# Mixer arithmetic moved from GpSimd to VectorE, up to the queries of a hybrid decoder layer

## The chip, the core and the metric

The kernel runs on one core of one Trainium2 chip. The metric is the device time of one execution in microseconds (us), lower is better. In the views of the profile PE is TensorE's matmul, PEld its weight load, DVE is VectorE, ACT is ScalarE, POOL is GpSimd, and SP is the queue that issues most DMAs. L191 is line 191 of the kernel before.

## What is computed

One decoder layer on 512 tokens of width 1,024, in float32. `c` is one vector that modulates the norms.

```python
mod = silu(c) @ w_ada + b_ada                      # six vectors of 1024
sh1, sc1, gt1, sh2, sc2, gt2 = split(mod, 6)
h = rms_norm(x, norm1_w) * (1 + sc1) + sh1
p = h @ w_in                                       # u, v; q, k, v, z; a, b
y_a = gelu(u) * spatial_gating(gelu(v))            # 8 heads, chunks of 128
q, k, v = silu(short_conv(p_q, p_k, p_v))          # 4 taps, then l2 norm of q, k
y_b = rms_norm(gated_delta_rule(q, k, v, g(a), beta(b))) * silu(z)   # 4 heads
x = x + gt1 * (concat(y_a, y_b) @ w_out)
h2 = rms_norm(x, norm2_w) * (1 + sc2) + sh2
x = x + gt2 * peer(h2)     # queries, keys, top 16, 128^2 single-neuron experts
out = rms_norm(x, final_norm_w)
```

The delta rule is computed chunkwise. Each chunk of 128 tokens needs the inverse of a unit triangular matrix for each of four heads.

## The kernel before, in words

Activations lie transposed, 128 channels on the partitions and 512 tokens along the row, eight such tiles for the width of 1,024. Every projection is made of three matmuls per tile: a float32 operand is split into an upper part (`hi`, a rounding cast on ScalarE) and a remainder (`lo = full - hi`, `split_lo`, L83), and `mm3` (L78 to L80) adds hi x hi, lo x hi and hi x lo. `weights` (L125) loads a block of 128 output columns as 128 x 1,024, casts it on ScalarE (L129) and forms the remainder on GpSimd unless another engine is named. Three buffers each hold `raw`, `whi` and `wlo`.

The stages, in order:

- *First norm* (L206 to L274). VectorE makes seven level masks `lvl` with 28 small instructions, adds up squares, and reduces sixteen rows of `w_ada` against silu(c) (`mod_sums`, L201, tiles of 128 x 1,024 called `wada`, eight buffers). The inverse root comes back as one row `rr`, the same on all partitions. GpSimd multiplies `xT` by `rr` (L253). For each of the eight tiles two sums are advanced, VectorE adds the bias and forms a scale column and a shift column, ScalarE writes `hhi` and once more the same value unrounded (`full`), and `low_parts` forms `hlo`, on GpSimd for four of the eight tiles (`GPL`). VectorE's order is as written here; the other engines' order is the planner's.
- *Convolution stage* (L308 to L408). Twelve projections of q, k and v go through `conv_silu`: a ScalarE copy, one L189 and three L191 on VectorE, a silu. Between them stand `lengths` (transposes and sums of squares, L354), the decay scalars (L325 to L339) and `decays` (`ml` and `att` on GpSimd, `LS` on VectorE). The order of TensorE is written by hand (`ORD`); the planner orders VectorE, ScalarE, GpSimd and the DMAs.
- *Chunk comparison* (L412 to L434): the triangular matrices `LS` and the attention matrices `att`, four chunks, between them the rest of the projections of v.
- *Levels of the inverse* (L446 to L471). Seven levels; per level and chunk a masked product `ms` on GpSimd (L451), then `py`, `pz`, `px` on TensorE and the updates of `X` and `Z` on VectorE. Thirty of the remaining 32 sums of `w_ada` are put among them, with two `wada` buffers.
- *Delta rule, gating and output projection* (L477 to L658), with `kd`, `sd`, the normed heads `on` and the masked gating weights on GpSimd; remainders of the mixed tiles alternate between VectorE and GpSimd (`split_mixed`).
- *Second norm* (L668 to L694): for tiles 2, 4 and 6 ScalarE scales `x2T` first (`pre`) and GpSimd multiplies by the row; the other tiles take one VectorE instruction.
- *Queries, routing and experts* from L763 on. The queries' weight remainders stay where they are, on GpSimd but for two.

Of the kernel before, what the change touches and what calls it, by code (L numbers as in the profile page):

```python
# [10 lines left out]
F32 = mybir.dt.float32  # L11
# [9 lines left out]
P = 128  # L21
D = 1024
S = 512
# [18 lines left out]
LATE = 1  # L42
ORD = "q1 l0 k2 q2 d l1 k3 l2 q3 f l3".split()
PRE2 = (2, 4, 6)
# [6 lines left out]
GPL = (2, 4, 5, 6)  # L51
# [8 lines left out]
def layer(ctx: ExitStack, tc: tile.TileContext, I, out):  # L60
# [64 lines left out]
    def weights(pl, src, n, eng=None):  # L125
        raw = pl.tile([P, KD, n], F32, tag="raw", name="raw")
        nc.sync.dma_start(raw, src)
        hi = pl.tile([P, KD, n], F32R, tag="whi", name="whi")
        nc.scalar.copy(hi, raw)  # L129
        lo = pl.tile([P, KD, n], F32R, tag="wlo", name="wlo")  # L130
        split_lo(eng or nc.gpsimd, lo, raw, hi)
        return hi, lo

# [9 lines left out]
    with ExitStack() as mixer:  # L143
# [52 lines left out]
        def mod_sums(which, wad, dst, base=0):  # L196

            for c in which:
                w = wad.tile([P, D], F32, tag="wada", name="wada")
                nc.sync.dma_start(w, I["w_ada_c"][c])  # L200
                nc.vector.tensor_tensor_reduce(w, w, scB, scale=1.0, scalar=0.0, op0=OP.mult, op1=OP.add,  # L201
                                               accum_out=dst[:, c - base:c - base + 1])
# [3 lines left out]
        with ExitStack() as n1, tc.manual_schedule(engines={nc.vector.engine}):  # L206
            for l in range(7):
                nc.vector.tensor_scalar(sj, pi, l, None, op0=OP.logical_shift_right)
                nc.vector.tensor_scalar(si, fi, l, 1, op0=OP.logical_shift_right, op1=OP.bitwise_xor)
                same = zT[:, 0, :P]  # L210
                nc.vector.tensor_tensor(same, si, sj, op=OP.is_equal)
                nc.vector.scalar_tensor_tensor(lvl[:, l], same, -1.0, m2[:, 0], op0=OP.mult, op1=OP.mult)
# [5 lines left out]
            wk0 = weights(wst, I["w_in_t"][4], P)  # L218
            ahead = mod_sums([8 * (1 - i) + k for k in range(KD) for i in range(2)], wad, mod)
# [16 lines left out]
            wq0 = weights(wst, I["w_in_t"][0], P, nc.vector)  # L236
# [4 lines left out]
            split_lo(nc.gpsimd, wlo, raw, whi)  # L241
            if not LATE:
                advance(ahead, 2)
# [8 lines left out]
            for k in range(KD):  # L252
                nc.gpsimd.tensor_tensor(xT[:, k], xT[:, k], rr, op=OP.mult)  # L253
                if k == 1:
                    wk1 = weights(wst, I["w_in_t"][5], P)
            fulls = []

            def low_parts(k):
                split_lo(nc.gpsimd if k in GPL else nc.vector, hlo[:, k], fulls[k], hhi[:, k])

            for k in range(KD):
                scale, shift = sc[:, k:k + 1], mod[:, k:k + 1]
# [12 lines left out]


        with ExitStack() as gdn, tc.manual_schedule(engines={nc.tensor.engine}):
# [90 lines left out]
            def decays(n):  # L368

                ml, ex = X[n], Y[n]  # L370
                nc.gpsimd.tensor_tensor(ml, bc(later[:, None, :], HP), col(g, n), op=OP.mult)
# [5 lines left out]
                nc.gpsimd.tensor_tensor(att[n], ex, bc(m2[:, 1:2], HP), op=OP.mult)  # L377
# [816 lines left out]
```

## Time and profile before

| | |
|---|---|
| median of 3 runs | 1,665.87 us (1,664.70 to 1,669.69) |
| profiled execution | 1,667.16 us, its span 1,665.5 us |
| PE busy | 1,567.7 us, 94% of the span |
| DVE busy | 1,311.7 us, 79% |
| ACT busy | 647.2 us, 39% |
| POOL busy | 662.6 us, 40% |

The span is the time from the first to the last instruction of the profiled execution. Busy shares are averages over stages that have different limits; the matmuls' ends are modelled, and they overlap, so that starts tell more than ends. In a row of the timeline stand start, length, engine, line, operation, output and inputs, the count, and in brackets how long the engine had been idle and what ended that.

### The profile page before, as it was taken

To read this page: it belongs to the slowest core of one execution; us is meant where nothing else is said; L and a number is where in the kernel's file an instruction comes from. 1 tells how busy PE (TensorE), PEld (TensorE's weight loads), DVE (VectorE), ACT (ScalarE), POOL (GpSimd) and SP (SyncE) were. 2 spreads that over 40 slices of the span, in tenths; PEclk is the share of its full clock that TensorE was granted. 3 is DMA by queue.
4 is the path that set the end of the run, shared out by engine and by line. 5 is a ranking of instruction groups with operands and counts; after the bars stand their busy time and mean duration, and the time that the engine had idled before them with its cause. 6 is when DMAs were issued, how large, how long until landed. Compare 5 with 4: busy or idle time off the path is not lost.

```text
span 1665.5 us, 23058 instructions
## 1 busy us (share of the span) xinstructions
PE 1567.7 (94%) x8567; PEld 1382.2 (83%) x8567; DVE 1311.7 (79%) x2388; ACT 647.2 (39%) x931; POOL 662.6 (40%) x454
## 2 busy tenths in 40 slices
PE   4889989999998889997999999999999999999996
PEld 2568988877888889986888888888888888888884
DVE  9889872545999999983688887888888888887755
ACT  4542123435335545553333333333333333333333
POOL 5455543426435610001244444445444444544201
PEclk9989999999999999998999999999999999999998
DMA  7311561236204457777889999999999999999753
GB/s 283 122 65 55 193 207 51 89 111 208 88 26 140 150 192 284 274 267 263 301 312 340 346 349 318 339 349 353 310 352 328 361 330 328 350 355 317 245 188 124
DMA packets 133396, 402.31 MB, mean 242 GB/s; under 512 B 12450, under 2 KB 49186, under 8 KB 131619
## 3 DMA queue, kind: packets, MB, share of 16 engines
q1 hardware_dynamic: 95106, 261.89, 44.0%
q0 software_dynamic: 38176, 138.95, 23.8%
q8 instruction: 67, 1.10, 0.3%
q14 instruction: 47, 0.38, 0.1%
HBM read 362.19 MB, written 38.60 MB: 241 GB/s over the span
## 4 chain that ended last, share of the span: by engine, by line
PE 79%; DVE 11%; DMA 4%; ACT 3%; issue 2%; POOL 1%; SPq 0%; DVEq 0%; ACTq 0%; POOLq 0%
PE pS L78 10%; PE pS L80 10%; PE acc L79 10%; PE acc L80 10%; PE pS L79 10%; PE acc L78 10%; DVE wada L201 3%; PE pp L79 2%; PE pp L78 2%; PE pp L80 2%; DMA wada<-in_w_ada_c 2%; PE pq L80 2%; PE pq L79 2%; PE pq L78 2%; DVE tmp L191 2%
## 5 line engine op out<-in xcount | busy, mean ns | idle before, releaser
L977 POOL DMA_INDIRECT u_rows<-in_u_rows,rows x128 | 204.8, 1600 | 561.8 <-DVE dots L984 341.1
L78 PE MATMUL pS<-hhi,uhi 128*128 128x384 f32 x1024 | 356.3, 348 | 1.1 <-ACT uhi L736 1.1
L80 PE MATMUL pS<-hhi,ulo 128*128 128x384 f32 x1024 | 349.0, 341 | 7.6 <-POOL ulo L83 7.6
L79 PE MATMUL pS<-hlo,uhi 128*128 128x384 f32 x1024 | 348.0, 340 | 0.0
L78 PE MATMUL acc<-vhi,ahi 128*128 128x512 f32 x768 | 300.8, 392 | 14.9 <-ACT vhi L1040 14.8
L79 PE MATMUL acc<-vlo,ahi 128*128 128x512 f32 x768 | 302.0, 393 | 1.7 <-DVE vlo L83 1.7
L80 PE MATMUL acc<-vhi,alo 128*128 128x512 f32 x768 | 302.2, 393 | 0.0
L80 PEld LDWEIGHTS pS<-hhi,ulo 128*128 128x128 f32 x1024 | 193.6, 189 | 8.8 <-POOL ulo L83 8.8
L78 PEld LDWEIGHTS pS<-hhi,uhi 128*128 128x128 f32 x1024 | 193.6, 189 | 4.9 <-ACT uhi L736 1.8
L79 PEld LDWEIGHTS pS<-hlo,uhi 128*128 128x128 f32 x1024 | 194.0, 189 | 3.7
L83 DVE TENSOR_TENSOR vlo<-vraw,vhi 128x1024 fp32r<-128x1024 f32 x128 | 156.7, 1225 | 50.0 <-ACT vhi L1040 50.0
L1027 ACT CAST ahi<-a 128x384 fp32r<-128x384 f32 x128 | 65.7, 513 | 333.6 <-DVE a L1025 333.6
L78 PEld LDWEIGHTS acc<-vhi,ahi 128*128 128x128 f32 x768 | 145.2, 189 | 44.5 <-ACT vhi L1040 16.0
L977 POOL DMA_INDIRECT v_rows<-in_v_rows,rows x128 | 148.5, 1160 | 74.0 <-issue 35.7
L83 POOL TENSOR_TENSOR wlo<-raw,whi 128x1024 fp32r<-128x1024 f32 x45 | 110.4, 2455 | 163.3 <-ACT whi L129 144.1
L79 PEld LDWEIGHTS acc<-vlo,ahi 128*128 128x128 f32 x768 | 145.0, 189 | 31.8 <-DVE vlo L83 3.0
L80 PEld LDWEIGHTS acc<-vhi,alo 128*128 128x128 f32 x768 | 145.0, 189 | 30.4
L994 DVE SCALAR_TENSOR_TENSOR facc<-v_rows,dots,facc 128x1024 f32<-128x1024 f32 x128 | 164.5, 1285 | 0.6
L984 DVE CUSTOM_DVE_ANT_0 junk<-u_rows,h2tok 128x1024 bf16<-128x1024 f32 x128 | 156.0, 1219 | 0.1
L736 ACT CAST uhi<-uraw 128x1024 fp32r<-128x1024 f32 x128 | 133.6, 1047 | 37.6 <-PE pS L79 36.3
L756 ACT ACTIVATE sgl<-pS 128x384 f32<-128x384 f32 x128 | 62.7, 490 | 217.2 <-PE pS L80 215.0
L1040 ACT CAST vhi<-vraw 128x1024 fp32r<-128x1024 f32 x128 | 133.9, 1047 | 0.0
(328 smaller groups left out, 2662.4 us busy)
## 6 DMA issues: line engine op xcount, KB each, us to landing
uraw<-in_u_t SPq DMA_DIRECT2D x128, 512.0 KB, 6.2
vraw<-in_v_rows SPq DMA_DIRECT2D x125, 512.0 KB, 5.9
wada<-in_w_ada_c SPq DMA_DIRECT2D x48, 512.0 KB, 3.4
gd<-scs SPq DMA_DIRECT2D x12, 2048.0 KB, 6.6
gates<-gd SPq DMA_DIRECT2D x16, 1536.0 KB, 12.6
raw<-in_w_in_t SPq DMA_DIRECT2D x24, 512.0 KB, 3.3
sgd<-sgl SPq DMA_DIRECT2D x47, 192.0 KB, 3.9
sgr<-sgd SPq DMA_DIRECT2D x47, 192.0 KB, 5.9
```

What stands on the lines that cost most here:

```text
L78: mm(o, ahi, bhi, start=start, stop=False)
L79: mm(o, ahi, blo, start=False, stop=False)
L80: mm(o, alo, bhi, start=False, stop=stop)
L83: eng.tensor_tensor(lo, full, hi.bitcast(F32), op=OP.subtract)
L201: nc.vector.tensor_tensor_reduce(w, w, scB, scale=1.0, scalar=0.0, op0=OP.mult, op1=OP.add, accum_out=dst[:, c - base:c - base + 1])
L736: nc.scalar.copy(hi, raw)
L756: nc.scalar.activation(sgl, pS[:, :TD], AF.Gelu_apprx_tanh)
L977: nc.gpsimd.indirect_dma_start(out=r, out_offset=None, in_=I[src], in_offset=bass.IndirectOffsetOnAxis(ap=rows_[:, j:j + 1], axis=0))
L984: nc.vector.tensor_tensor_reduce(junk, rowsin.pop(("u_rows", j)), h2tok, scale=1.0, scalar=0.0, op0=OP.mult, op1=OP.add, accum_out=dots[j ...
L994: nc.vector.scalar_tensor_tensor(facc, rowsin.pop(("v_rows", j)), d[:, j % GP:j % GP + 1], facc, op0=OP.mult, op1=OP.add)
L1027: nc.scalar.copy(ahi, a)
L1040: nc.scalar.copy(hi, raw)
```

## The change

GpSimd does no elementwise arithmetic any more up to the queries, apart from one column of 4 elements. The weight remainders of the mixer, the masks (`ml`, `att`, `ms`, the gating weights), the products (`kd`, `sd`, `on`, the second norm's `xn`) and half of the mixed remainders go to VectorE, at the same places of the program. The remainders of the queries' weights stay as they were, and so do GpSimd's memsets and selects at the start.

The first norm is written anew. The bias of `mod` is the start value of the sum, so that the column additions go; the scale column is one ScalarE instruction; `xn = xT * scale * rr` is one VectorE instruction per tile, and the low part takes `xn + shift - hhi` in one. `full` and the pass that wrote it go. The weights that are loaded early are split in two steps, so that VectorE's remainder of each has a place of its own in the written order. The 28 instructions for `lvl` stand behind the norm instead of ahead of it. `kd`, `sd`, `on` and the gating weights change their engine in the same way as the lines shown.

```diff
-LATE = 1
-PRE2 = (2, 4, 6)
-GPL = (2, 4, 5, 6)
...
-    def weights(pl, src, n, eng=None):
+    def upper_weights(pl, src, n):
         raw = pl.tile([P, KD, n], F32, tag="raw", name="raw")
         nc.sync.dma_start(raw, src)
         hi = pl.tile([P, KD, n], F32R, tag="whi", name="whi")
         nc.scalar.copy(hi, raw)
-        lo = pl.tile([P, KD, n], F32R, tag="wlo", name="wlo")
-        split_lo(eng or nc.gpsimd, lo, raw, hi)
+        return raw, hi
+
+    def both_weights(pl, raw, hi, eng=None):
+        lo = pl.tile(list(raw.shape), F32R, tag="wlo", name="wlo")
+        split_lo(eng or nc.vector, lo, raw, hi)
         return hi, lo
+
+    def weights(pl, src, n, eng=None):
+        return both_weights(pl, *upper_weights(pl, src, n), eng)
...
-        def mod_sums(which, wad, dst, base=0):
+        def mod_sums(which, wad, dst, base=0, bias=None):
...
-                nc.vector.tensor_tensor_reduce(w, w, scB, scale=1.0, scalar=0.0, op0=OP.mult, op1=OP.add,
-                                               accum_out=dst[:, c - base:c - base + 1])
+                nc.vector.tensor_tensor_reduce(w, w, scB, scale=1.0, scalar=0.0 if bias is None else bias[:, c:c + 1], op0=OP.mult,
+                                               op1=OP.add, accum_out=dst[:, c - base:c - base + 1])
                 yield
...
         with ExitStack() as n1, tc.manual_schedule(engines={nc.vector.engine}):
-            for l in range(7):
-                nc.vector.tensor_scalar(sj, pi, l, None, op0=OP.logical_shift_right)
...
-            wk0 = weights(wst, I["w_in_t"][4], P)
-            ahead = mod_sums([8 * (1 - i) + k for k in range(KD) for i in range(2)], wad, mod)
+            wk0 = upper_weights(wst, I["w_in_t"][4], P)
+            ahead = mod_sums([8 * (1 - i) + k for k in range(KD) for i in range(2)], wad, mod, bias=b_ada)
...
-            wq0 = weights(wst, I["w_in_t"][0], P, nc.vector)
+            wq0 = upper_weights(wst, I["w_in_t"][0], P)
...
-            split_lo(nc.gpsimd, wlo, raw, whi)
-            if not LATE:
-                advance(ahead, 2)
+            advance(ahead, 2)
+            wk0 = both_weights(wst, *wk0)
+            split_lo(nc.vector, wlo, raw, whi)
...
+            xns = []
+
+            def modulated(k):
+
+                scale, shift = sc[:, k:k + 1], mod[:, k:k + 1]
+                nc.scalar.activation(scale, mod[:, 8 + k:9 + k], AF.Identity, bias=n1w[:, k:k + 1], scale=n1w[:, k:k + 1])
+                xns.append(nrm.tile([P, S], F32, tag="xn", name="xn", bufs=3))
+                nc.vector.scalar_tensor_tensor(xns[k], xT[:, k], scale, rr, op0=OP.mult, op1=OP.mult)
+                nc.scalar.activation(hhi[:, k], xns[k], AF.Identity, bias=shift)
+
+            def low_parts(k):
+                nc.vector.scalar_tensor_tensor(hlo[:, k], xns[k], mod[:, k:k + 1], hhi[:, k].bitcast(F32), op0=OP.add, op1=OP.subtract)
+
             for k in range(KD):
-                nc.gpsimd.tensor_tensor(xT[:, k], xT[:, k], rr, op=OP.mult)
-                if k == 1:
-                    wk1 = weights(wst, I["w_in_t"][5], P)
...
-                if k >= 2 - LATE:
-                    advance(ahead, 2)
-                nc.vector.tensor_tensor(scale, mod[:, 8 + k:9 + k], b_ada[:, 8 + k:9 + k], op=OP.add)
-                nc.vector.scalar_tensor_tensor(scale, scale, 1.0, n1w[:, k:k + 1], op0=OP.add, op1=OP.mult)
-                nc.vector.tensor_tensor(shift, shift, b_ada[:, k:k + 1], op=OP.add)
-                full = nrm.tile([P, S], F32, tag="full", name="full", bufs=3)
-                fulls.append(full)
-                nc.scalar.activation(hhi[:, k], xT[:, k], AF.Identity, bias=shift, scale=scale)
-                nc.scalar.activation(full, xT[:, k], AF.Identity, bias=shift, scale=scale)
-                if k:
-                    low_parts(k - 1)
-            low_parts(KD - 1)
+                modulated(k)
+                if k == 0:
+                    wk1 = upper_weights(wst, I["w_in_t"][5], P)
+                    wq0 = both_weights(wst, *wq0)
+                advance(ahead, 2)
+                low_parts(k)
+                if k == 0:
+                    wk1 = both_weights(wst, *wk1)
+            for l in range(7):
+                nc.vector.tensor_scalar(sj, pi, l, None, op0=OP.logical_shift_right)
+                nc.vector.tensor_scalar(si, fi, l, 1, op0=OP.logical_shift_right, op1=OP.bitwise_xor)
+                same = zT[:, 0, :P]
+                nc.vector.tensor_tensor(same, si, sj, op=OP.is_equal)
+                nc.vector.scalar_tensor_tensor(lvl[:, l], same, -1.0, m2[:, 0], op0=OP.mult, op1=OP.mult)
...
-                nc.gpsimd.tensor_tensor(ml, bc(later[:, None, :], HP), col(g, n), op=OP.mult)
+                nc.vector.tensor_tensor(ml, bc(later[:, None, :], HP), col(g, n), op=OP.mult)
...
-                nc.gpsimd.tensor_tensor(att[n], ex, bc(m2[:, 1:2], HP), op=OP.mult)
+                nc.vector.tensor_tensor(att[n], ex, bc(m2[:, 1:2], HP), op=OP.mult)
...
-                    nc.gpsimd.tensor_tensor(ms, LS[n], bc(lvl[:, l:l + 1, :], HP), op=OP.mult)
+                    nc.vector.tensor_tensor(ms, LS[n], bc(lvl[:, l:l + 1, :], HP), op=OP.mult)
...
-                split_lo(nc.vector if k % 2 else nc.gpsimd, mlo[k], src, mhi[k])
+                split_lo(nc.vector, mlo[k], src, mhi[k])
...
-                    if c in PRE2:
-                        pre[c] = o1.tile([P, S], F32, name=f"pre{c}")
-                        nc.scalar.mul(pre[c], x2T[:, c], sc[:, KD + c:KD + c + 1])
...
-                if k in pre:
-                    nc.gpsimd.tensor_tensor(xn, pre[k], rr, op=OP.mult)
-                else:
-                    nc.vector.scalar_tensor_tensor(xn, x2T[:, k], sc[:, KD + k:KD + k + 1], rr, op0=OP.mult, op1=OP.mult)
+                nc.vector.scalar_tensor_tensor(xn, x2T[:, k], sc[:, KD + k:KD + k + 1], rr, op0=OP.mult, op1=OP.mult)
...
-            nc.gpsimd.tensor_tensor(last, h2hi[:, :, TD:].bitcast(F32), h2lo[:, :, TD:].bitcast(F32), op=OP.add)
+            nc.vector.tensor_tensor(last, h2hi[:, :, TD:].bitcast(F32), h2lo[:, :, TD:].bitcast(F32), op=OP.add)
```

## Rows read from the trace of the kernel before

**Rows 1.** Busy time of each engine by stage: stretch, its length, engines, granted clock, DMA.

```profile
core 0: us, PE busy (x) PEld busy (x) DVE busy (x) ACT busy (x) POOL busy (x), PEclk, DMA share, GB/s
15.80:57.30 41.50, 27.17 (x100) 17.87 (x101) 39.56 (x63) 13.97 (x19) 24.07 (x14) 1.00 0.62 229
57.30:127.25 69.95, 58.05 (x256) 45.95 (x255) 59.23 (x134) 36.81 (x55) 34.80 (x17) 0.90 0.21 68
127.25:157.70 30.45, 26.84 (x176) 24.27 (x176) 27.98 (x55) 7.54 (x10) 15.55 (x9) 0.95 0.16 52
157.70:226.90 69.20, 64.42 (x545) 63.22 (x545) 58.99 (x96) 14.07 (x24) 40.96 (x24) 0.97 0.56 188
245.40:382.10 136.70, 131.88 (x732) 110.66 (x730) 56.82 (x89) 53.88 (x76) 55.72 (x29) 1.00 0.29 96
```

**Rows 2.** Timeline of DVE, then of POOL, where the first convolutions run.

```profile
59.62 2.28 DVE L189 TENSOR_SCALAR tmp<-tmp,cols 128x512 f32<-128x512 f32 x1 [2.39 <-ACT tmp L188]
61.94 5.58 DVE L191 SCALAR_TENSOR_TENSOR tmp<-tmp,cols 128x511 f32<-128x511 f32 x2
67.44 0.47 DVE L189 TENSOR_SCALAR tmp<-tmp,cols 128x512 f32<-128x512 f32 x1
67.83 1.40 DVE L191 SCALAR_TENSOR_TENSOR tmp<-tmp,cols 128x509 f32<-128x509 f32 x2
...
59.24 7.73 POOL L83 TENSOR_TENSOR wlo<-raw,whi 128x1024 fp32r<-128x1024 f32 x3 [4.57 <-ACT whi L129]
```

**Rows 3.** Timeline of the first norm, one ACT row, then DVE.

```profile
10.85 1.07 ACT L223 ACTIVATE sq<-xT 128x1024 f32<-128x1024 f32 x1
...
13.11 2.72 DVE L226 TENSOR_TENSOR sq<-sq 128x512 f32<-128x512 f32 x1
...
36.23 0.68 DVE L83 TENSOR_TENSOR hlo<-full,hhi 128x512 fp32r<-128x512 f32 x1
36.83 1.22 DVE L201 CUSTOM_DVE_ANT_0 wada<-wada,h2tok 128x1024 f32<-128x1024 f32 x1
...
56.54 0.69 DVE L83 TENSOR_TENSOR hlo<-full,hhi 128x512 fp32r<-128x512 f32 x1 [1.59 <-ACT full L271]
```

**Rows 4.** Timeline of DVE: first and last of the 28 instructions that make `lvl`.

```profile
2.60 0.24 DVE L208 TENSOR_SCALAR uT<-uT 128x128 int32<-128x128 int32 x1 [2.60 <-POOL uT L160]
...
8.93 0.29 DVE L212 SCALAR_TENSOR_TENSOR lvl<-zT,m 128x128 f32<-128x128 f32 x1
```

**Rows 5.** Groups by line, 59.6 to 127.2 us, DVE (busy us, mean ns, idle before).

```profile
L191 DVE SCALAR_TENSOR_TENSOR tmp<-tmp,cols 128x511 f32<-128x511 f32 (+2 forms) x27 | 28.6, 1072 | 0.4
L189 DVE TENSOR_SCALAR tmp<-tmp,cols 128x512 f32<-128x512 f32 x9 | 11.4, 1272 | 6.7 <-ACT tmp L188 6.7
L334 DVE TENSOR_TENSOR po<-po,s 128x16 f32<-128x16 f32 x7 | 5.6, 802 | 0.1
...
L336 DVE TENSOR_TENSOR po<-po,s 128x16 f32<-128x16 f32 x1 | 0.2, 174 | 0.0
```

**Rows 6.** Timeline of PE: a stop in the convolution stage and matmuls behind it.

```profile
118.08 1.12 PE L349 MATMUL pks<-ident,qT 128*128 128x128 f32 x4 [3.12 <-ACT qT L192]
...
119.42 0.63 PE L79 MATMUL pp<-hlo,whi 128*128 128x512 f32 x1
...
123.69 0.44 PE L80 MATMUL pp<-hhi,wlo 128*128 128x512 f32 x1
...
126.54 0.40 PE L80 MATMUL pp<-hhi,wlo 128*128 128x512 f32 x1
```

**Rows 7.** A PE wait at 155.7 us; groups of 157.7 to 227 us, DVE and POOL.

```profile
155.72 2.07 PE L454 MATMUL py<-ident,ms 128*128 128x128 f32 x8 [3.61 <-POOL ms L451]
...
L201 DVE CUSTOM_DVE_ANT_0 wada<-wada,h2tok 128x1024 f32<-128x1024 f32 x25 | 42.8, 1714 | 9.9 <-DMA wada<-in_w_ada_c 9.7
...
L451 POOL TENSOR_TENSOR ms<-ls,lvl 128x512 f32<-128x512 f32 x23 | 40.2, 1776 | 17.5 <-PE py L454 17.3
```

**Rows 8.** Timeline of DVE: the first two products of the second norm.

```profile
378.16 3.26 DVE L691 SCALAR_TENSOR_TENSOR xn<-x2T,sc,rr 128x512 f32<-128x512 f32 x2 [1.18 <-ACT rr L683]
```

More of the change, by code (lines that the diff above doesn't have):

```diff
@@ L200, in mod_sums @@
                 nc.sync.dma_start(w, I["w_ada_c"][c])
-                nc.vector.tensor_tensor_reduce(w, w, scB, scale=1.0, scalar=0.0, op0=OP.mult, op1=OP.add,
-                                               accum_out=dst[:, c - base:c - base + 1])
+                nc.vector.tensor_tensor_reduce(w, w, scB, scale=1.0, scalar=0.0 if bias is None else bias[:, c:c + 1], op0=OP.mult,
+                                               op1=OP.add, accum_out=dst[:, c - base:c - base + 1])
                 yield
         with ExitStack() as n1, tc.manual_schedule(engines={nc.vector.engine}):
-            for l in range(7):
-                nc.vector.tensor_scalar(sj, pi, l, None, op0=OP.logical_shift_right)
[L209 to L212, printed above, removed]
             wad = n1.enter_context(pool("wad", 8))
@@ L251, in layer @@
             nc.gpsimd.tensor_scalar(nega, nega, -1.0, None, op0=OP.mult)
-            for k in range(KD):
-                nc.gpsimd.tensor_tensor(xT[:, k], xT[:, k], rr, op=OP.mult)
-                if k == 1:
-                    wk1 = weights(wst, I["w_in_t"][5], P)
[L256 to L262, printed above, removed]
-                if k >= 2 - LATE:
-                    advance(ahead, 2)
-                nc.vector.tensor_tensor(scale, mod[:, 8 + k:9 + k], b_ada[:, 8 + k:9 + k], op=OP.add)
-                nc.vector.scalar_tensor_tensor(scale, scale, 1.0, n1w[:, k:k + 1], op0=OP.add, op1=OP.mult)
-                nc.vector.tensor_tensor(shift, shift, b_ada[:, k:k + 1], op=OP.add)
-                full = nrm.tile([P, S], F32, tag="full", name="full", bufs=3)
-                fulls.append(full)
-                nc.scalar.activation(hhi[:, k], xT[:, k], AF.Identity, bias=shift, scale=scale)
-                nc.scalar.activation(full, xT[:, k], AF.Identity, bias=shift, scale=scale)
-                if k:
-                    low_parts(k - 1)
@@ L507, in token_kv @@
                     kd = t4("kd")
-                    nc.gpsimd.tensor_tensor(kd, kr, col(krk, n), op=OP.mult)
+                    nc.vector.tensor_tensor(kd, kr, col(krk, n), op=OP.mult)
                 tok[n] = (vb, kbe, kd)
@@ L540, in layer @@
                         sd = t4("sd")
-                        nc.gpsimd.tensor_tensor(sd, state, col(eg[:, 2], n), op=OP.mult)
+                        nc.vector.tensor_tensor(sd, state, col(eg[:, 2], n), op=OP.mult)
                         nc.vector.tensor_tensor(new, sd, heads(pst), op=OP.add)
@@ L575, in layer @@
                 on = att[n]
-                nc.gpsimd.tensor_tensor(on, raw_o[n], col(ro, n), op=OP.mult)
+                nc.vector.tensor_tensor(on, raw_o[n], col(ro, n), op=OP.mult)
                 ons.append(on)
@@ L583, in layer @@
                 nc.sync.dma_start(X[i], I["gm_ws_t"][:, 4 * i:4 * i + 4])
-                nc.gpsimd.tensor_tensor(X[i], X[i], bc(upper[:, None, :], HP), op=OP.mult)
+                nc.vector.tensor_tensor(X[i], X[i], bc(upper[:, None, :], HP), op=OP.mult)
             bsr = X[3]
@@ L640, in layer @@
             sqs = o1.tile([P, S], F32, name="sqs")
-            pre = {}
             def residual(c):
@@ L777, in query @@
                     with tc.high_priority(QPR):
-                        hi, lo = weights(q2, I["wq_t"][c], P, nc.vector if c in QV else None)
+                        hi, lo = weights(q2, I["wq_t"][c], P, nc.vector if c in QV else nc.gpsimd)
                 else:
-                    hi, lo = weights(q2, I["wq_t"][c], P, nc.vector if c in QV else None)
+                    hi, lo = weights(q2, I["wq_t"][c], P, nc.vector if c in QV else nc.gpsimd)
                 pq = stream("pq")
```

## The prediction

> **What bounds the kernel now.** I read the busy time by stage first, because the change ends at the queries and the average over 1,665 us says nothing of that part. In the first norm, up to 57.3 us, VectorE is busy 39.56 of 41.50 us and TensorE 27.17. In the convolution stage, to 127.25 us, TensorE's granted clock averages 0.90 of full, so it stops and starts. In the levels of the inverse, from 157.7 us, TensorE is busy 64.42 of 69.20 us, and from 245.4 us to the queries 131.88 of 136.70 us [rows 1]. So the first two stages can give time, the third little, the rest almost none; behind the queries nothing is edited.
>
> Then the timeline of the full stage, because busy time isn't work. One convolution runs L189 once and L191 three times. While GpSimd works through three weight remainders (59.24 to 66.97 us), L189 takes 2.28 us and two of L191 5.58 us; right after, the same instructions take 0.47 us and 1.40 us for two [rows 2]. The reader is to see that VectorE is "busy" for four times its work when a GpSimd instruction runs beside it. The groups put a size on it: in the convolution stage 27 of L191 average 1.072 us against 0.70 us free, nine of L189 1.272 us against 0.47, seven of L334 0.802 us against 0.174 for the like L336 [rows 2, 5]. That is 27 x 0.37 + 9 x 0.80 + 7 x 0.63 = 10.0 + 7.2 + 4.4 = 21.6 us of VectorE time that is waiting.
>
> **The change, part by part.** All prices are those of instructions that nothing disturbs. A 512-wide product or remainder takes 0.68 us, and the next instruction starts 0.60 us after it did; a 1,024-wide sum takes 1.22 us, with the same overlap 1.15 from start to start [rows 3]. I take 1.15 for a 1,024-wide remainder too, an estimate from equal width.
>
> *First norm.* The last addition of squares ends at 15.83 us, 2.72 us long. Its input is there at 11.92 us; with two additions of 0.6 and 0.7 us it ends at 13.2 us [rows 3]. Behind it VectorE's written order has four sums (4.6), the reciprocal (0.2), `wk0`'s remainder (1.15), the narrow one (0.1): 19.2 us. Then xn(0) 0.6, `wq0`'s remainder 1.15, two sums 2.3, low(0) 0.6, `wk1`'s remainder 1.15: 25.0 us. Steps 1 to 5 are xn, two sums, low part, 3.5 us each: 42.5 us. Steps 6 and 7 have no sums left, so each is a chain: scale column on ScalarE 0.2 (an estimate, like VectorE's smallest, [rows 5]), xn 0.6, hhi 0.8 (an estimate: ScalarE's 1,024-wide pass takes 1.07, [rows 3]), low part 0.6, together 2.2 us: 46.9 us. Before, the last low part ends at 57.2 us [rows 3]. The column additions go (the bias starts the sum), the second pass over `full` goes, and the scale column moves to ScalarE, which is busy 13.97 of 41.50 us [rows 1].
>
> *The 28 `lvl` instructions* move from 2.60 to 9.2 us, where their neighbours waited for ScalarE, to behind the last low part: 6.6 us [rows 4]. The first convolution could start 2.4 us behind the last low part, as before (57.2 to 59.6, [rows 2, 3]); that cover hides 2.4 and the rest is paid. It starts at 53.5 us, against 59.6: **6.1 us earlier**.
>
> *Convolution stage.* Of VectorE's 59.2 busy us [rows 1] the 21.6 go, and 15.2 come: nine remainders at 1.15 (on GpSimd three took 7.73, [rows 2]) and eight 512-wide products (`ml`, `att`) at 0.60. That makes 52.8. From 59.6 to 127.25 us VectorE also idles 67.6 - 59.2 = 8.4 us for ScalarE and TensorE; I keep that. So 53.5 + 52.8 + 8.4 = 114.7 us, **12.5 us earlier** than 127.25, the norm's 6.1 included. Bounds: with no idle time left, 20.9; with the convolution part giving nothing, 6.1.
>
> *Chunk comparison, 127.25 to 157.7 us.* TensorE waits 3.61 us for `ms`, which stands on GpSimd behind a weight remainder [rows 7]. On VectorE it follows its `ls`; but VectorE is busy 27.98 of 30.45 us [rows 1]. Between 0 and 3.6; I take **2**.
>
> *Levels.* The 25 sums average 1.714 us and would take 1.22: 12.3 us go. The 23 `ms` come at 0.68: 15.6 [rows 3, 7]. VectorE's 59.0 becomes 62.3, and with its 9.9 us of waits for `wada` transfers 72.2, 3.0 over the stage. TensorE's idle time there is 4.8 us [rows 1]. Between -3.0 and +4.8; I take the middle, **1**. Behind a sum that waits for its transfer now also stand the `ms`, and TensorE waits for those.
>
> *Up to the queries.* `kd`, `sd`, the head products, the masked weights and half of the mixed remainders cost VectorE 0.6 each, and the weights 1.15; I cost them at nothing, since VectorE is busy 56.82 of 136.70 us there under a full TensorE [rows 1]. Without that cover, the remainders of the sixteen projections of u, v and the output alone would cost 16 x 1.15 = 18 us. In the second norm the first two xn take 3.26 us where two free ones take 1.3, one blocked by a weight remainder that stays on GpSimd and one by an xn that goes [rows 8]: **1**, bounds 0 and 2. No DMA is added or moved to another queue.
>
> The sum is 12.5 + 2 + 1 + 1 = 16.5 us. The profiled execution took 1,667.2 us (span 1,665.5), 1.3 above the median of the runs: 1,665.9 - 16.5 = 1,649.4, say **1,649 us**.
>
> **A rule beside the rows.** The rows show the slow instructions only beside GpSimd's [rows 2]. The Trainium skill, SBUF — State Buffer, "Who interferes with whom", says that a VectorE instruction with two inputs in SBUF, or in a two-port mode, and a GpSimd instruction that reads SBUF shut each other out for the whole instruction. By it all 21.6 us return, as in my sum. [...]
>
> **The rivals.**
> *More returns (1,634 to 1,640).* VectorE's idle time in the convolutions goes too, since some of it is the echo of late convolutions: 20.9 + 3.6 + 4.8 + 2 = 31 us. For it: TensorE waits for `qT`, which waits for convolutions [rows 6]. Against: ScalarE's table loads and round trips stay.
> *Only the norm pays (1,660).* The convolution stage goes by the chain from TensorE over ScalarE and VectorE and back, and freed VectorE time turns to idle: 6.1 us stay; 1,663 with the levels' loss. Against: VectorE is busy 59.2 of 67.6 us.
> *Weights come late (slower, 1,674).* GpSimd took each remainder as soon as ScalarE was done; on VectorE it waits its turn behind convolutions, and TensorE stops. A stop of 3.1 us costs more: the ten matmuls from 119.42 us start 0.43 us apart, the twelve from 123.69 us 0.24, so the clock stood at the lower of its two levels, 1.2 GHz, for 10 x 0.19 = 1.9 us of loss [rows 6]. A stop is then 5 us. The sum's 16.5 us are gone from the fourth stop beyond today's; five make 25 - 16.5 = +8.5. Against: weights have three buffers.
> *Nothing moves (1,666).* The 6.1 us are used up by later waits in the order written for TensorE.
> *The times are true lengths (slower, 1,683).* If GpSimd's work did not lengthen VectorE's, the convolutions would take 53.5 + 59.2 + 15.2 + 8.4 = 136.3 us, 9 later, and the levels 15.6 - 4.8 = 11 longer, less the 2 and 1 elsewhere: +17. Against it speaks the same instruction at both lengths within 6 us [rows 2].
>
> **Chances.** My forecast 0.60, its own range 1,640 to 1,657; more returns 0.12; only the norm 0.15, about two thirds of it below 1,661; late weights 0.06; nothing moves 0.05; true lengths 0.02. A measurement of this kernel tells 0.3% (5 us) from no change. Faster: 0.60 + 0.12 + 0.10 = 0.82. Same: 0.05 + 0.05 = 0.10. Slower: 0.08. The range goes from 1,634, the upper bounds together, to 1,662, near the lower ones; it leaves out the slower cases, nothing moves, and the ends of the others.
>
> **What the profile after would show.** L191 at 0.70 us and L189 at 0.47 all through; sums at 1.22; the last low part near 47 us and `lvl` until 53.5; the first `prb` matmul near 115 us, with fewer matmuls at half clock; the levels as long as before within 4 us; the queries starting some 16 us earlier and all behind them as long as before. Wrong would make it: TensorE waiting for `wlo` from VectorE in the convolutions; VectorE waiting for `wada` in the norm, where no such wait shows now and where the sums would ask for their sixteen half-megabytes within 29 us; or `ms` held behind late sums.

## The result and the profile after

The changed kernel takes 1,649.39 us (1,648.68 to 1,649.67, four runs) beside 1,666.95 us for the kernel before (four runs): a ratio of 0.9893, 95% interval 0.9876 to 0.991. The forecast of 1,649 us was right to a microsecond, but its terms were not: that their sum came so near is luck. The spans of the two profiled executions are 1,647.0 and 1,665.5 us, 18.5 apart:

| stretch | term of the prediction | measured |
|---|---|---|
| to the first convolution | 6.1 | 59.62 - 53.15 = 6.5 |
| to the first `prb` matmul (the end of the convolution stage), the first row included | 12.5 | 127.25 - 109.37 = 17.9 |
| chunk comparison | 2 | 30.45 - 34.10 = -3.65 |
| levels | 1 | 69.20 - 65.99 = 3.2 |
| from there to the queries | 1 | 153.66 - 156.33 = -2.7 |
| behind the start of the queries | 0 | 18.5 - 14.8 = 3.7 |

The windows by stage of the changed kernel answer to [rows 1] (length, then busy time of PE, PEld, DVE, ACT and POOL, the granted clock, DMA):

```profile
13.40:48.80 35.40, 26.53 (x96) 17.88 (x97) 33.82 (x55) 11.54 (x21) 0.00 (x0) 1.00 0.74 299
53.15:109.37 56.22, 49.53 (x243) 40.55 (x241) 50.94 (x164) 35.25 (x54) 0.00 (x0) 0.97 0.26 85
109.37:143.47 34.10, 26.94 (x177) 24.27 (x177) 30.82 (x70) 7.20 (x10) 0.00 (x0) 0.94 0.14 47
143.47:209.46 65.99, 64.66 (x545) 64.08 (x545) 59.00 (x115) 14.09 (x24) 0.00 (x0) 0.95 0.65 213
209.46:365.79 156.33, 148.65 (x819) 125.11 (x817) 80.53 (x147) 55.37 (x78) 2.43 (x1) 0.99 0.30 100
```

GpSimd is at zero in these rows, but for one remainder of the queries' weights (2.43 us). In the convolution stage VectorE is still the fullest engine, 50.94 of 56.22 us, but what it does is work now. The groups of that stage, DVE (busy us, mean ns, idle before), answer to [rows 5]; L194 and L192 are the old L191 and L189:

```profile
L194 DVE SCALAR_TENSOR_TENSOR tmp<-tmp,cols 128x511 f32<-128x511 f32 (+2 forms) x27 | 20.1, 745 | 0.1
L80 DVE TENSOR_TENSOR wlo<-raw,whi 128x1024 fp32r<-128x1024 f32 x8 | 9.7, 1219 | 2.2 <-ACT whi L126 2.2
L192 DVE TENSOR_SCALAR tmp<-tmp,cols 128x512 f32<-128x512 f32 x9 | 4.2, 472 | 1.3 <-ACT tmp L191 1.3
L336 DVE TENSOR_TENSOR po<-po,s 128x16 f32<-128x16 f32 x7 | 1.2, 173 | 0.0
```

The reader is to see the means: 745 ns for 1,072, 472 for 1,272, 173 for 802. The idle time ahead of L192, 6.7 us before, is down to 1.3, and 2.2 us of waiting for `whi` has come.

The loss is in the chunk comparison. The timeline of PE in the changed kernel shows two stops for `ms`, and behind them 32 matmuls of the same form at two lengths:

```profile
139.37 2.07 PE L456 MATMUL py<-ident,ms 128*128 128x128 f32 x8 [5.14 <-DVE ms L453]
143.47 6.75 PE L456 MATMUL py<-X,ms 128*128 128x128 f32 x32 [2.02 <-DVE ms L453]
...
157.20 3.74 PE L456 MATMUL py<-X,ms 128*128 128x128 f32 x32
```

What stands ahead of those `ms` in VectorE's order is seen in its timeline:

```profile
138.63 0.69 DVE L453 TENSOR_TENSOR ms<-ls,lvl 128x512 f32<-128x512 f32 x1
139.23 1.22 DVE L204 CUSTOM_DVE_ANT_0 wada<-wada,h2tok 128x1024 f32<-128x1024 f32 x1
...
140.97 1.22 DVE L204 CUSTOM_DVE_ANT_0 wada<-wada,h2tok 128x1024 f32<-128x1024 f32 x1
...
142.12 0.69 DVE L458 TENSOR_TENSOR X<-py,ident 128x512 f32<-128x512 f32 x1
142.72 1.29 DVE L453 TENSOR_TENSOR ms<-ls,lvl 128x512 f32<-128x512 f32 x2
```

From 131.40 to 143.47 us VectorE has no gap: it is busy 12.07 of 12.07 us. The granted clock between 143.47 and 150.05 us is 0.54, the lower of the two levels, after a stretch in which TensorE was busy 4.91 of 12.07 us; at 157.20 it is 1.00. So the stops cost 3.0 us once more in the levels (6.75 - 3.74). The kernel before paid 1.8 us there, behind its stop of 3.61 us; its timeline of PE:

```profile
157.73 5.51 PE L454 MATMUL py<-X,ms 128*128 128x128 f32 x32
```

### The profile page after: what moved, and what is told of

Read it like the earlier page. It is cut to its first block, busy times and chain, and to the rows that moved or that the text cites. A ratio compares the mean times of both kernels' runs of the same rounds, so it can differ in the third digit from the quotient of the medians.

```text
span 1647.0 us, 22971 instructions
## 1 busy us (share of the span) xinstructions
PE 1564.7 (95%) x8567; PEld 1382.6 (84%) x8567; DVE 1308.4 (79%) x2463; ACT 642.7 (39%) x928; POOL 478.8 (29%) x355
## 4 chain that ended last, share of the span: by engine, by line
PE 81%; DVE 10%; DMA 5%; ACT 2%; issue 1%; POOL 1%; SPq 0%; DVEq 0%; ACTq 0%; POOLq 0%
PE pS L75 10%; PE acc L76 10%; PE acc L77 10%; PE pS L77 10%; PE acc L75 10%; PE pS L76 10%; DMA wada<-in_w_ada_c 3%; PE pp L76 3%; PE pp L75 3%; PE pp L77 3%; DVE wada L204 2%; PE pq L76 2%; PE pq L77 2%; PE pq L75 2%; PE pgb L915 1%
## 5 line engine op out<-in xcount | busy, mean ns | idle before, releaser
L80 POOL TENSOR_TENSOR wlo<-raw,whi 128x1024 fp32r<-128x1024 f32 x14 | 33.7, 2408 | 393.7 <-PE ptx L661 358.8
```

The lines of the kernel that those rows point to most:

```text
L80: eng.tensor_tensor(lo, full, hi.bitcast(F32), op=OP.subtract)
```

## The experiments

Each was timed beside the kernel before on its own chip; ratios are to that kernel, with 95% intervals. The changed kernel's own is 0.9893 (0.9876 to 0.991).

### How large the shut-out is, and what makes it

**Unused remainders on GpSimd.** The changed kernel, with GpSimd forming each remainder of the convolution stage's weights too, into a place that nobody reads:

```diff
         raw, hi = upper_weights(pl, src, n)
+        if idle is not None:
+            nc.gpsimd.tensor_tensor(idle, raw, hi.bitcast(F32), op=OP.subtract)
```

> The changed kernel, and in the projections of the convolutions GpSimd forms each weight remainder once more, into a place that nobody reads. No engine waits for it. Theory (GpSimd's instructions shut VectorE's out): the nine remainders of some 2.4 us lengthen what VectorE does beside them; L191's like in the convolution stage goes from 0.745 us mean to over 0.95, the first prb matmul from 109.4 us to 120 or later, the time to 1,660 (1,657 to 1,667). Rival (the gain is one of order and of waits for GpSimd's queue): work that nobody waits for costs nothing, 1,649 within 2 us.

1,670.91 us, ratio 1.002 (1.001 to 1.003): the whole gain is gone, by work that nobody waits for. The loss is larger than expected, and it does not fall where it was expected: L194's like stayed at 742 ns instead of going over 950. The stage from the first convolution to `prb` takes 73.36 us for 56.22, VectorE's busy time in it 67.75 for 50.94. Timeline of POOL, then of DVE, in that kernel (its L197 and L277 to L281 are the changed kernel's L192 and L272 to L276):

```profile
51.57 8.40 POOL L137 TENSOR_TENSOR uT<-raw,whi 128x1024 f32<-128x1024 f32 x3 [48.26 <-ACT whi L126]
```
```profile
51.59 1.22 DVE L80 TENSOR_TENSOR wlo<-raw,whi 128x1024 fp32r<-128x1024 f32 x1
52.73 2.50 DVE L280 TENSOR_TENSOR zT<-uT 128x128 f32<-128x128 int32 x1
55.15 2.63 DVE L197 TENSOR_SCALAR tmp<-tmp,cols 128x512 f32<-128x512 f32 x1
57.70 2.42 DVE L281 SCALAR_TENSOR_TENSOR lvl<-zT,m 128x128 f32<-128x128 f32 x1
60.05 0.21 DVE L277 TENSOR_SCALAR uT<-uT 128x128 int32<-128x128 int32 x1
...
60.98 0.28 DVE L280 TENSOR_TENSOR zT<-uT 128x128 f32<-128x128 int32 x1
```

Three instructions on GpSimd, three on VectorE that are long, one beside each, whatever their own length is (0.28 and 0.47 us free). The sums of the rows fit taking turns: 8.40 us is the 1.14 of VectorE's remainder and three times 2.4. So here VectorE's price for a remainder on GpSimd is nearly the remainder's own length, once: 16.8 us more busy time for the eight in the window, 2.1 each, where GpSimd is busy 20.73 us, 2.6 each.

**Memsets instead.** As above, but behind a remainder of one column, three memsets:

```diff
-            nc.gpsimd.tensor_tensor(idle, raw, hi.bitcast(F32), op=OP.subtract)
+            nc.gpsimd.tensor_tensor(idle[:, 0, :1], raw[:, 0, :1], hi[:, 0, :1].bitcast(F32), op=OP.subtract)
+            for _ in range(3):
+                nc.gpsimd.memset(idle, 0.0)
```

> The changed kernel with GpSimd kept as busy as in the run with idle remainders, but without reading: behind each of the same nine casts one remainder of a single column, then three unused memsets of 128x1,024 (0.96 us each in the changed kernel), 26 us in all. They only write. Theory (what lengthens VectorE's instructions is a GpSimd instruction that reads tensors, not GpSimd being busy): VectorE's L192 form stays near 0.47 us against 1.14 with the idle remainders, first prb at 107 to 111, time 1,649 (1,646 to 1,653). Rival (any GpSimd instruction of that length shuts VectorE out): first prb at 125 to 130, time 1,668 to 1,673. Between the two, a part of it: the shut-out is by the ports that both use, in proportion.

1,654.95 us, ratio 0.9913 (0.9893 to 0.9933), first `prb` at 114.10: neither end. By the first `prb` it is a quarter of the loss (4.7 of 19.1 us); in the time the intervals do not part it from the changed kernel. Timeline of POOL, then of DVE beside those memsets (L199, L201 and L279 to L283 are the changed kernel's L192, L194 and L272 to L276):

```profile
52.30 1.27 POOL L137 TENSOR_TENSOR uT<-raw,whi 128x1 f32<-128x1 f32 x1 [49.02 <-ACT whi L126]
53.63 3.17 POOL L139 MEMSET uT<- 128x1024 f32 x3
```
```profile
53.64 1.22 DVE L199 TENSOR_SCALAR tmp<-tmp,cols 128x512 f32<-128x512 f32 x1
54.78 0.28 DVE L283 SCALAR_TENSOR_TENSOR lvl<-zT,m 128x128 f32<-128x128 f32 x1
54.98 0.86 DVE L279 TENSOR_SCALAR uT<-uT 128x128 int32<-128x128 int32 x1
55.12 0.79 DVE L280 TENSOR_SCALAR uT<-uT 128x128 int32<-128x128 int32 x1
55.83 0.73 DVE L201 SCALAR_TENSOR_TENSOR tmp<-tmp,cols 128x511 f32<-128x511 f32 x1
```

Beside a GpSimd instruction that only writes, VectorE's instructions with two tensors as inputs keep their length (0.28, 0.73), and those with one can be held (1.22 for 0.47, 0.8 for 0.22). Not each is: the nine of L199 in the stage average 695 ns, for 472 undisturbed. So the loss is not by GpSimd being busy, and not by reading alone.

### The parts of the change

**The first norm alone**, put into the kernel before; the remainders and masks stay on GpSimd, `lvl` moves as in the change:

```diff
-                nc.gpsimd.tensor_tensor(xT[:, k], xT[:, k], rr, op=OP.mult)
...
+                nc.vector.scalar_tensor_tensor(xns[k], xT[:, k], scale, rr, op0=OP.mult, op1=OP.mult)
...
+        return both_weights(pl, *upper_weights(pl, src, n), eng or nc.gpsimd)
```

> The kernel before with the rewritten first norm alone (its remainders on VectorE, lvl behind it); everything behind the norm stays on GpSimd. Theory: the first convolution starts 6 us earlier, the convolution stage keeps its length of 67.6 us because its VectorE is still shut out, and the time is 1,660 (1,657 to 1,663). Rival (the norm makes most of the gain, later stages follow): 1,649 to 1,654.

1,663.52 us, ratio 0.9968 (0.9952 to 0.9984). First convolution at 54.14, first `prb` at 122.47, 4.8 earlier than before: the norm's gain of 5.5 at the first convolution is mostly kept through the stage and to the end (5.3 us by the ratio, for the 6 expected; the time itself lies half a microsecond above its range).

**The mixer's weight remainders back on GpSimd**, behind the norm, everything else as in the change:

```diff
-        return both_weights(pl, *upper_weights(pl, src, n), eng)
+        return both_weights(pl, *upper_weights(pl, src, n), eng or nc.gpsimd)
```

> The changed kernel with all weight remainders behind the norm back on GpSimd; masks and products stay on VectorE. Theory: the convolution stage wins 9 x 1.15 = 10 us of VectorE work and loses about 9 x 2.1 = 19 us to being shut out, so +6 to +9 there, nothing in the stages that TensorE bounds: 1,657 (1,653 to 1,661). Rival (masks and products made the gain, remainders are free on GpSimd): 1,645 to 1,650.

1,662.9 us, ratio 0.9965 (0.9953 to 0.9977). First `prb` at 122.82, 13.4 later than in the changed kernel. With the norm's 4.8 these make 18.2 of the stage's 17.9 us: the norm and the remainders carry it, and the other edits together leave no mark in its time beyond the scatter of 2 us that is told below. The expected 1,657 was too small a loss, as in the run with idle remainders.

**`lvl` back in front of the norm**, with the change's other edits:

```diff
+            for l in range(7):
+                nc.vector.tensor_scalar(sj, pi, l, None, op0=OP.logical_shift_right)
...
             wad = n1.enter_context(pool("wad", 8))
...
-            for l in range(7):
-                nc.vector.tensor_scalar(sj, pi, l, None, op0=OP.logical_shift_right)
...
```

> The changed kernel with the 28 instructions that make lvl back in front of the first norm. Theory (VectorE's 6.6 us of lvl stand between the last low part and the first convolution, and are paid there): the first convolution starts 3 to 5 us earlier than 53.15, the first prb matmul 3 to 5 us earlier than 109.37, and the time falls to 1,645 (1,643 to 1,647). Rival (the convolution stage goes by the chain over ScalarE and TensorE, so an earlier VectorE turns into idle time): first prb within 1 us of 109.4, time 1,648 to 1,651. Other rival (in front they delay the additions of squares): the last low part ends later than 48.84 by up to 6 us, and the time is 1,649 or above.

1,653.05 us, ratio 0.992 (0.9907 to 0.9934): no gain, rather a loss, and none of the three forecasts came. Timeline of DVE between the norm and the first convolution, with nothing of `lvl` there:

```profile
48.38 0.75 DVE L266 SCALAR_TENSOR_TENSOR hlo<-xn,mod,hhi 128x512 fp32r<-128x512 f32 x1 [0.79 <-ACT hhi L263]
52.03 1.23 DVE L80 TENSOR_TENSOR wlo<-raw,whi 128x1024 fp32r<-128x1024 f32 x1 [2.90 <-ACT whi L126]
53.18 0.48 DVE L192 TENSOR_SCALAR tmp<-tmp,cols 128x512 f32<-128x512 f32 x1
```

The convolution starts at the same 53.2 us: it stands behind a remainder (1.23 us) for whose cast VectorE idles 2.90 us, and the cast waited for the projections on TensorE. What `lvl` took was idle time; the stage with it in front is 58.15 us long for 56.22, and VectorE waits 7.8 us in it for `whi`, 2.2 in the changed kernel. These 2 us are no more than the scatter told below; why the levels take 3 us more, where the sums wait 10.4 us for transfers instead of 6.2, stays open.

### The chunk comparison and the levels

**`ms` back on GpSimd**, and then only that of levels 0 and 1:

```diff
-                    nc.vector.tensor_tensor(ms, LS[n], bc(lvl[:, l:l + 1, :], HP), op=OP.mult)
+                    nc.gpsimd.tensor_tensor(ms, LS[n], bc(lvl[:, l:l + 1, :], HP), op=OP.mult)
...
+                    (nc.vector if l > 1 else nc.gpsimd).tensor_tensor(ms, LS[n], bc(lvl[:, l:l + 1, :], HP), op=OP.mult)
```

> The changed kernel with the level products ms back on GpSimd, all else as changed. Theory: the sums among them are lengthened again (1.22 to 1.6 us or more) and the levels take 69 us in place of 66, but the chunk comparison gets back the 3.6 us that it lost, since ms no longer waits its turn on VectorE: 1,649 within 3 us. Rival (ms on VectorE gains in the levels and the loss ahead of them has another cause): 1,652 to 1,655.

> The changed kernel with the level products ms of levels 0 and 1 alone on GpSimd, the other five levels on VectorE. Theory (ms on VectorE loses in the chunk comparison, which VectorE bounds, 30.8 busy of 34.1 us, and gains in the levels, 66.0 us against 70.3 with all of ms on GpSimd): the chunk comparison, first prb to first py with X, takes 28 to 29.5 us, the levels 66 to 67.5, the levels end at 204 to 206.5, time 1,643 (1,640 to 1,646). Rival (the two parts do not add, since a sum lengthened beside a level-1 product costs as much as it saves): levels 69 us or more, time 1,646 to 1,650.

All of `ms`: 1,644.04 us, ratio 0.9858 (0.9835 to 0.988); levels 0 and 1: 1,641.99 us, ratio 0.984 (0.9826 to 0.9854). The first missed both its forecasts, being faster than either; the second came as expected but for the end of its levels, at 203.46. Windows of the chunk comparison and the levels, all of `ms` on GpSimd, then levels 0 and 1:

```profile
109.48:137.49 28.01, 26.02 (x177) 23.46 (x177) 24.31 (x58) 7.19 (x10) 6.41 (x6) 1.00 0.11 38
137.49:207.76 70.27, 65.63 (x544) 64.54 (x545) 56.49 (x93) 14.07 (x24) 41.72 (x23) 0.95 0.58 189
```
```profile
107.97:136.49 28.52, 26.60 (x177) 24.23 (x177) 24.46 (x58) 7.20 (x10) 6.93 (x6) 0.97 0.11 38
136.49:203.46 66.97, 62.85 (x545) 62.00 (x545) 59.17 (x113) 14.06 (x24) 3.39 (x3) 0.99 0.60 197
```

Moving `ms` to VectorE cost 6.1 us in the chunk comparison (34.10 against 28.01) and gave 4.3 in the levels (65.99 against 70.27), where on GpSimd they lengthen the sums to 1,587 ns, from 1,224. One instruction, two stages, opposite signs. The two make 1.8 of the 4.0 us by which the profiled spans differ; most of the rest lies in the stretch up to the queries (153.9 for 156.3), in which nothing was edited.

**Level 0's `ms` right behind its `ls`**, ahead of the products `at`; nothing added or removed:

```diff
                         nc.vector.scalar_tensor_tensor(dst[:, h], src[:, h * P:(h + 1) * P], rk[:, n, h:h + 1], dst[:, h], op0=OP.mult, op1=OP.mult)
+                    if dst is LS[n]:
+                        ms0[n] = g2.tile(HP, F32, tag="ms", name="ms", bufs=4)
+                        nc.vector.tensor_tensor(ms0[n], dst, bc(lvl[:, 0:1, :], HP), op=OP.mult)
```

> The changed kernel with the product ms of level 0 formed right behind the products ls that it reads, ahead of the four products at and of the next chunk's work; nothing is added or removed. Theory (the stop of 5.14 us before the last py with the identity comes from ms standing behind at, X and Z in VectorE's written order): the stop shrinks to 3 us or less, first py with X 2 to 4 us before 143.47, time 1,646 (1,644 to 1,648). Rival (VectorE, busy 30.8 of 34.1 us in the chunk comparison, is itself the limit, and the order moves the wait elsewhere): first py with X within 1 us of 143.5, time 1,648 to 1,651.

1,644.2 us (1,643.2 to 1,650.15), ratio 0.9876 (0.9856 to 0.9896), which the interval does not part from the changed kernel. The time fits the theory, and the first `py` with X comes at 141.73, but the first `prb` came 1.7 us earlier too. The trace decides, for the rival's mechanism and not for its figures: the stop of 5.14 us shrinks to 1.37, a stop of 6.71 us comes one matmul group later, and the chunk comparison is 34.09 us long for 34.10.

```profile
133.86 1.16 PE L460 MATMUL py<-ident,ms 128*128 128x128 f32 x8 [1.37 <-DVE ms L431]
141.73 0.58 PE L460 MATMUL py<-X,ms 128*128 128x128 f32 x1 [6.71 <-DVE ms L457]
```

The place of level 0's `ms` isn't the cause. That it is the amount of work that VectorE has up to the first level-1 product, two sums included, is borne out where some of it is taken away: 28.5 us with the `ms` of levels 0 and 1 on GpSimd, 31.9 without the sums (below).

**The later sums out of the levels.** Written into the delta-rule loop only, alone and then together with `ms` on GpSimd and `lvl` in front:

```diff
-                    if l:
-                        advance(later_sums, 1 if n else 2)
...
-                advance(fill, 13)
+                for _ in range(13):
+                    advance(fill, 1)
+                    advance(later_sums, 1)
```

> The changed kernel with the 32 later sums over the ada weights taken out of the levels and put into the delta-rule loop, one behind each step of its filling work. Theory (the level products ms on VectorE come late because they stand behind sums, some of which wait for a transfer): TensorE's wait of 2.02 us for ms before the first py with X goes, so do the half-clock matmuls behind it (32 py in 6.75 us against 3.74 us later on), and the end of the levels comes 4 to 7 us earlier than 209.46; VectorE, busy 68.8 of 139 us up to the queries, takes the 40 us of sums there under a full TensorE; time 1,643 (1,641 to 1,646). Rival (it is the amount of VectorE work around the first levels, not the sums): end of levels within 2 us of 209.5, time 1,648 or above. Other rival (the sums, beside GpSimd's work in the delta rule or waiting for transfers, hold up VectorE there): levels earlier, but the queries start no earlier than 366 us, time 1,649 to 1,653.

> The changed kernel with three edits: lvl made in front, the later sums in the delta-rule loop, and the level products ms on GpSimd. Theory (the last took 5 us off the changed kernel and cost it only in the levels, where it lengthened the sums, 1,558 ns against 1,224; with no sums there the cost is gone, and lvl in front gives 3 to 5 us): end of levels near 201 us, time 1,637 (1,634 to 1,641). Rival (GpSimd's products, beside the additions into X and Z, hold up the levels even without sums): end of levels 204 us or later, time 1,641 to 1,646. If the sums hurt in the delta rule, the levels are early but the queries start no earlier than 360 us.

1,645.9 us, ratio 0.9875 (0.986 to 0.989), and 1,647.14 us, ratio 0.9878 (0.9863 to 0.9893). The second missed its forecasts (1,637, rival 1,641 to 1,646). The first time is as expected, but by another road: nothing held the sums back, and the planner put ten of them among the convolutions. Groups of the convolution stage, DVE, of the first of the two:

```profile
L204 DVE CUSTOM_DVE_ANT_0 wada<-wada,h2tok,cols 128x1024 f32<-128x1024 f32 x10 | 12.6, 1277 | 0.0
```

The stage takes 66.03 us for 56.22, first `prb` at 119.63; in the second, 65.00. That VectorE's load sets this stage is so shown once more: 12.6 us of sums, some 10 us of time. The levels with only 17 sums take 61.67 us.

**The sums held behind the levels by their data**, alone and with `ms` of levels 0 and 1 on GpSimd. They stand in the delta-rule loop as in the runs before, and their start value is made from the last `Z`:

```diff
+            start = t4("msum")[:, 0, :48]
+            nc.vector.scalar_tensor_tensor(start, Z[NT - 1][:, 0, :48], 0.0, b_ada, op0=OP.mult, op1=OP.add)
+            later_sums = mod_sums(range(16, 48), wad, mod, 0, start)
```

> The changed kernel with the 32 later sums over the ada weights held behind the levels by their data: their start value is the bias plus zero times a column of the last Z. Nothing ahead of the first sum changes its place, and the convolution stage is as in the changed kernel. Theory (in the levels the ms, X and Z stand behind sums that wait for transfers, 6.2 us in all, and two sums stand ahead of the first level-1 product): first prb as before at 109.4, first py with X at 140 to 142.5, levels 61.5 to 63 us, end of the levels at 202 to 205; VectorE takes the 40 us of sums under the full TensorE up to the queries, time 1,643 (1,640 to 1,646). Rival (the sums hold up VectorE in the delta rule): the levels end early, but the queries start at 365 us or later, time 1,648 or above. Other rival (the wait for ms is VectorE's amount of work, and the levels are as long without sums): end of the levels at 208 or later.

> Both of the other two edits: ms of levels 0 and 1 on GpSimd, and the 32 later sums held behind the levels. Theory (the two costs are separate): first py with X at 137 to 138.5, levels 61.5 to 64 us, their end at 199 to 202, time 1,639 (1,636 to 1,643). Rival (both edits remove the same wait): end of the levels 203 or later, time no better than the better of the two.

Alone 1,638.72 us, ratio 0.9822 (0.9808 to 0.9835); with both edits 1,635.36 us, ratio 0.9797 (0.9784 to 0.9811), the best of all, 34 us below the kernel before on the same chip, and by the ratios 16 below the changed one. Both are a little faster than the ranges expected, and the levels end 1.1 us earlier than expected, as the first `prb` came earlier (107.6 for 109.4). Windows of the chunk comparison, the levels and the stretch up to the queries, alone, then both:

```profile
107.65:139.51 31.86, 26.72 (x176) 24.35 (x177) 28.57 (x66) 7.19 (x10) 0.00 (x0) 0.97 0.10 34
139.51:200.94 61.43, 61.43 (x546) 61.43 (x546) 35.99 (x73) 14.08 (x24) 0.00 (x0) 0.99 0.10 32
200.94:355.88 154.94, 148.71 (x819) 125.26 (x817) 109.17 (x193) 55.15 (x78) 2.45 (x1) 0.99 0.56 183
```
```profile
107.55:135.95 28.40, 26.48 (x176) 24.11 (x177) 24.45 (x58) 7.19 (x10) 6.80 (x6) 0.98 0.12 38
135.95:197.86 61.91, 61.91 (x546) 61.82 (x546) 37.26 (x73) 14.07 (x24) 3.62 (x3) 0.98 0.10 31
197.86:349.63 151.77, 147.06 (x818) 123.93 (x816) 109.03 (x192) 55.23 (x78) 2.45 (x1) 1.00 0.57 187
```

Without the sums TensorE is busy through all of the levels, 61.43 of 61.43 us. Thirty of them come in the next stretch, and it is no longer than in the changed kernel (154.94 against 156.33): they lie in VectorE's idle time there. The two edits add: 28.40 and 61.91 in one kernel.

In the kernels compared, the first `prb` lies at 107.6 to 109.5 us where nothing ahead of it was edited; a shift of 2 us is therefore not read as an effect. The stretch from the levels' end to the queries scatters more: where nothing in it was edited (the changed kernel, all of `ms` or that of levels 0 and 1 on GpSimd, `lvl` in front, the early `ms`) it takes 151.7 to 157.1 us, and no run here shows what sets it.

## Why the prediction was right or wrong, point by point

**The main step was right, and shown.** VectorE's long instructions were waits for GpSimd: with GpSimd's work taken away they are short, and with it put back, as remainders that nobody reads, it costs some 21 us (ratio 1.002 for 0.9893). The rival of true lengths is ruled out. The Trainium skill, SBUF — State Buffer, "Who interferes with whom", says that a two-input VectorE instruction collides only with a GpSimd instruction that reads, and one in a two-port mode with any; by the memsets the trace agrees on the first (0.73 us kept), and on the second (0.47 became 1.22) if that instruction ran in such a mode, which no row shows. The Trainium skill's Perfetto Trace Analysis, "Optimizing Scalar/DVE Operations", says that with VectorE saturated it may make sense to give work to GpSimd, and that between these two it might not help. These runs show both: for the remainders it cost 13 us, for the `ms` in the chunk comparison it gained 6.

**First norm: right, with a wrong reason for one number.** The last low part ends at 48.84 us instead of 46.9, since the sum with a column as its start value takes 1.28 us, not 1.22, and the products with a column 0.75, not 0.68. Then I had let `lvl` pay 6.6 less 2.4 us, until 53.5; measured 53.15. With `lvl` in front it is 53.18: between the last low part and the convolution stand then a wait for a cast (2.90) and a remainder (1.23), so `lvl` was not paid for. The step that failed is "that cover hides 2.4 and the rest is paid"; two errors made a right number, by luck.

**Convolution stage: mis-sized, 17.9 for 12.5.** By the groups before and after, L191 gives back 8.5, L189 7.2, L334 4.4, as I had it within 1.5 (L191's free length is 0.745 us, not the 0.70 that I took from two that overlap); the sums of squares of `vn` (418 to 286 ns, 2.2 us) and `LS` (953 to 686 ns, 1.0 us) I had left out: 23.3 for 21.6. And "8.4 idle; I keep that" was wrong: 5.3 remain, the wait for `tmp` falling from 6.7 to 1.3 us while `whi` comes in with 2.2. The stage is 56.2 us long where I had 61.2: idle 3.1 less, busy 1.9 less. That is a part of the rival with more returns, its idle time as an echo of late convolutions; that it was one is argued from these rows, not shown by a run.

**Chunk comparison: the sign was wrong, -3.65 for +2.** The first wrong step was the reading that the last `ms` stood on GpSimd behind a weight remainder. The timeline of POOL in the kernel before shows that it waited for VectorE:

```profile
148.62 2.62 POOL L83 TENSOR_TENSOR wlo<-raw,whi 128x1024 fp32r<-128x1024 f32 x1
153.96 3.38 POOL L451 TENSOR_TENSOR ms<-ls,lvl 128x512 f32<-128x512 f32 x2 [2.72 <-DVE ls L426]
```

The remainder was done at 151.24, and GpSimd then idled 2.72 us for `ls`. So VectorE set the end of TensorE's stop before the change too. I had bounded it by 0 and 3.6, both gains, beside the sentence that VectorE is busy 27.98 of 30.45 us. I counted the wait that goes and not the work that comes: six `ms` (4.0 us), two remainders (2.4), two sums that now fall into this stretch (2.4) and three instructions on `X` and `Z` that do too (2.1), against 7 us that lengthened instructions give back (L191 3.0, L189 1.6, `Z` 2.4). With the six `ms` on GpSimd the stage takes 28.0 us, 2.4 less than before, so the forecast's 2 was there to be had by leaving them; with the two sums gone it takes 31.9. So a longer stop by VectorE took the place of the one that I had put down to GpSimd, which I had named as a danger for the levels alone.

**Levels: right in sign, 3.2 for 1.** The bound of 4.8 was TensorE's idle time, of which 1.3 are left (65.99 - 64.66). The bound of -3.0 kept VectorE's 9.9 us of waits for transfers as they were; they fell to 6.4. Of what could still go, 65.99 - 61.43 = 4.6 us, 3.0 are the matmuls at the lower clock behind the stops of the stage ahead. With the sums moved out all 4.6 go.

**Up to the queries: -2.7 for +1.** TensorE waits for `vb` (2.2 us) and `kbe` (1.9 us) behind late sums, in VectorE's order. But kernels that leave this stretch alone differ by 5 us in it, so that the loss itself is not shown to come from the change. The second norm's gain shows only behind the start of the queries: from the first `pq` matmul to the end of the scores it is 107.6 us, for 110.7 before and 111.1 in the run with the norm alone, which keeps the old second norm; it is 107.3 in the run with the mixer's remainders back on GpSimd, which has the new one. A stop of 1.6 us for `whi` and some matmuls at the lower clock are gone there.

**No weights came late,** as forecast: no wait of TensorE for `wlo` up to the queries is above 0.3 us, and VectorE does not wait for `wada` in the first norm. The third sign, `ms` held behind late sums, came, in the chunk comparison. The sum of 16.5 stands so near 18.5 because its errors cancel: 5.4 too little in the convolutions, 2.2 in the levels and 3.7 behind the queries' start, and 5.7 and 3.7 too much in between.

## What to carry to other kernels

Price work on GpSimd by what it does to VectorE: a weight remainder on GpSimd held VectorE for 2.1 of its 2.6 us here, though nobody waited for its result. When work is brought to VectorE, go stage by stage and ask in each whether VectorE has the time before the next engine's deadline: the same `ms` cost 6 us in one stage and gave 4 in the next. Work with a late deadline, like the sums, belongs where VectorE is idle; the planner here put ten of them into a full stage (10 us) until their data made them wait.

## What was not expected of the hardware

- The two engines take turns by whole instructions: beside three GpSimd remainders (8.40 us) exactly three VectorE instructions took 2.4 to 2.6 us, of 0.28 and 0.47 us free ones, and the 27 two-input products of the convolutions stayed at 742 ns.
- GpSimd memsets delayed one-input VectorE instructions (0.22 to 0.8 us, 0.47 to 1.22), though not each, and left the two-input ones at their length; a GpSimd remainder of a single column took 1.27 us beside a VectorE remainder of 1.22.
- The reduction with a column as its start value takes 1.28 us, for 1.22 with a constant (means of 1,277 to 1,283 ns in groups of such sums, 1,224 in the groups of the others).
